# A feed-forward gate by ScalarE's x times sigmoid function, with one GpSimd product less for each half, and the second weight unit's remainders on VectorE

## The chip, the cores and the metric

One core of one Trainium2 chip runs the whole program. The metric is the device time of one execution in microseconds; a profiled execution gives the trace. In the profile PE is TensorE (matmul), PEld its weight load, DVE is VectorE, ACT is ScalarE, POOL is GpSimd, and SP (SyncE) issues the DMAs.

## The reference

A layer of a streaming encoder on x of 1024 frames by 1024 features: a mixing part (a recurrent mixer and band attention), a feed-forward part and a last gated embedding. The change lies in the feed-forward part:

```python
h2 = rmsnorm(x, norm_ffn_g[li])
x = x + (jax.nn.silu(h2 @ w_ffn_gate[li]) * (h2 @ w_ffn_up[li])) @ w_ffn_down[li]
h3 = rmsnorm(x, norm_ple_g[li])
x = x + jax.nn.sigmoid(h3 @ w_ple_gate[li]) * (p[li].astype(x.dtype) @ w_ple_proj[li])
```

Here silu(a) is a times sigmoid(a), and the hidden width D_FF is 2816. All inputs and outputs are float32.

## The kernel before

Activations lie with features on the 128 partitions and the 1024 frames along the free axis; most tiles are 128 x 1024 or a half of that, 128 x 512. Each float32 operand of a matmul is split into a high part (a cast to the matmul's own 32-bit type, `hi`) and a remainder (`lo`, the operand minus `hi`), and each product is made of three matmuls: hi by hi, hi by lo, lo by hi. In the trace the high parts of weights are `whi` or `wh`, the remainders `wlo` or `wl`. A remainder of weights is made by `wrest(engine, w, src)`, a subtraction of two SBUF tiles on the engine that it is given.

The feed-forward gate and up products are done by a Winograd form of Strassen's algorithm. The hidden features are cut into 22 units of 256, a unit of gate weights and one of up weights by turns. A unit takes seven products (`product(0)` to `product(6)`), each 12 matmuls of 128 x 128 by 128 x 512, that go into three PSUM banks b1, b2 and b3; b2 and b3 get a second product added, so DVE has to read what is there first (the sums u2 and u3). The seven weight blocks a11, s21 (two of them), a12, s3 and s4 are made from the unit's two raw tiles r1 and r2 by sums on DVE (tiles q), casts on ACT and remainders on DVE or POOL:

- `first_weights` makes those of the first unit. `strassen_weights(engine=None)` makes those of every later one, in steps that the caller advances with `next(more)`. Inside it G is the engine that was given, or POOL; a11, a12, s3 and s4 have their remainders made on G, s21 on V (DVE).
- `first_part` runs products 0 to 3 of the first gate unit, and `second_part` its products 4, 6 and 5, with the second unit's weights made between them: `more = self.strassen_weights()`.
- `ff_pairs` then runs the other 21 units by `strassen`; a unit's side stream (`side`) makes the next unit's weights, stores earlier results and issues the loads.

Order is fixed: V, A and G are wrappers (`Pinned`) that put each instruction behind the one recorded before it on the same engine, and PE and the loads on SP are chained in the same way. An engine that waits therefore holds up all that was recorded behind it. Where an instruction is issued through `nc.scalar` or `nc.vector` directly, a scheduler places it.

`unit_gate(c, half, ps)` takes a finished 128 x 512 result of a gate unit. `self.rb` holds each frame's factor of the norm, on all partitions. It makes g = ps times rb on DVE, sigmoid(g) on ACT into a temporary s (`t` in the trace), and then on POOL g times s and that times rb (the second rb is the up product's norm factor, applied ahead). `unit_up` multiplies the up product into it on DVE. There are 44 calls of `unit_gate`: four in `second_part` and 40 in the loop. Since these helpers record through `Pinned`, nearly all their instructions have line L54 in the trace, and matmuls L83; tiles tell them apart.

Rows that the text below uses: `q<-wr,wr`, `q<-q,wr`, `q<-wr` and `q<-wr,q` are a unit's weight sums on DVE; `s<-pm,rb` and `s<-t,rb` on DVE are the first line of `unit_gate`; `t<-pm,t` are the sums u2 and u3; `t<-s` on ACT is the gate function; `s<-s,t` and `s<-s,rb` on POOL are the two products.

After the loop come the product with the down weights (`ff_down`) and the last gated embedding (`ple`), which uses ACT's sigmoid.

Of the kernel before, what the change touches and what calls it, by code (L numbers as in the profile page):

```python
# [13 lines left out]
AF = mybir.ActivationFunctionType  # L14
ALU = mybir.AluOpType
# [41 lines left out]
class Trunk:  # L57
# [1244 lines left out]
    def second_part(self):  # L1302

        V, A = self.V, self.A
        b1, b2, b3 = self.banks
        self.strassen_load()
        next(self.embedded)
        self.norm_sums()
        for i in range(2):
            self.ffn_cast("T4", i)  # L1310
        u3 = self.stmp()
        V.tensor_tensor(u3, b2, self.p1, ALU.add)
        V.tensor_tensor(u3, b3, u3, ALU.add)
        next(self.embedded)
        drain(self.firsts)
        for i in range(2):
            self.ffn_rest("T4", i)
        self.gu = [self.slot() for _ in range(2)]
        drain(self.embedded)
        self.norm_rows()  # L1320
        self.unit_gate(1, 0, u3)
        more = self.strassen_weights()
        next(more)
        next(more)
        self.product(4, self.blocks("B21"), b1, False)
        next(more)
        self.unit_gate(0, 1, b1)
        next(more)
        self.product(6, self.blocks("B22"), b3, False)
        next(more)  # L1330
        V.tensor_tensor(self.u2, b3, self.u2, ALU.add)
        self.unit_gate(0, 0, self.u2)
        self.product(5, self.blocks("T4"), b2, False)
        next(more)
        u = self.stmp()
        V.tensor_tensor(u, b2, self.p1, ALU.add)
        self.unit_gate(1, 1, u)
        drain(more)
        self.sops = [self.blocks(kind) for kind in ("B11", "T2", "T1", "T3", "B21", "T4", "B22")]
# [31 lines left out]
    def unit_gate(self, c, half, ps):  # L1371
        V, A, G = self.V, self.A, self.G
        g = self.gu[c]
        hs = slice(half * HALF, half * HALF + HALF)
        s = self.stmp()
        V.tensor_tensor(g[:, hs], ps, self.rb[:, hs], ALU.mult)
        A.activation(s, g[:, hs], AF.Sigmoid)
        G.tensor_tensor(g[:, hs], g[:, hs], s, ALU.mult)
        G.tensor_tensor(g[:, hs], g[:, hs], self.rb[:, hs], ALU.mult)

    def unit_up(self, c, half, ps):
        hs = slice(half * HALF, half * HALF + HALF)
# [537 lines left out]
def drain(stream):  # L1920
    while True:
        try:
            next(stream)
        except StopIteration as e:
            return e.value
# [114 lines left out]
```

## Time and profile before

| | |
|---|---|
| median of 3 runs | 1595.65 us (1594.68 to 1601.39) |
| profiled execution, its own time | 1595.63 us |
| span of that execution in the trace | 1593.7 us |
| granted TensorE clock, mean | 0.998 |
| busy: PE, DVE, POOL, ACT | 1566.2, 1171.8, 783.6, 643.7 us |
| bytes moved by DMA | 230.52 MB, mean 145 GB/s |

The span is the time from the first to the last instruction in the trace; the time of an execution is 1.9 us longer. Busy times of different engines overlap, so their sum means nothing; what counts is which engine the end waits for at each stage. A row of a timeline gives start, length, engine, line, operation, output<-inputs, shape, count, and in brackets how long the engine was idle before it and who released it. The length of an operation includes the time in which it has begun and cannot go on.

### The profile page before, as it was taken

The numbers are of one execution on the slowest core, as the hardware profiler recorded it, in microseconds if no ns is written. First come the engines' busy times: TensorE is split into PE (matmuls) and PEld (weight loads), VectorE is DVE, ScalarE is ACT, GpSimd is POOL, SyncE is SP. The second block draws the span as 40 slices with busy tenths as digits, with TensorE's granted clock in tenths as the row PEclk, the third lists the DMA queues.
The fourth block names the chain that finished last, engine by engine and source line by source line (L and its number), as shares of the span: only waits on it lengthen the run. The fifth ranks groups of instructions, "written<-read, shape, count | busy, mean of one in ns | idle before, by whom it ended". The sixth has DMA issues, their size and how long they took to land.

```text
span 1593.7 us, 21834 instructions
## 1 busy us (share of the span) xinstructions
PE 1566.2 (98%) x8224; PEld 1309.3 (82%) x8224; DVE 1171.8 (74%) x1767; ACT 643.7 (40%) x1089; POOL 783.6 (49%) x445
## 2 busy tenths in 40 slices
PE   8999999999999999999999999999999999999997
PEld 6998989877888888888887788888888888888886
DVE  5656765489998777544898988888888866765658
ACT  5321221167677633421377322232222234445453
POOL 3422221257563064325230777777777764644554
PEclk9999999999999999999999999999999999999999
DMA  5101100245663465475244422233333268875334
GB/s 191 54 28 41 40 28 27 100 146 174 224 245 107 143 192 187 146 285 210 80 141 177 152 99 99 100 99 109 103 108 108 80 255 322 304 278 189 126 134 157
DMA packets 81897, 230.52 MB, mean 145 GB/s; under 512 B 9216, under 2 KB 9984, under 8 KB 81280
## 3 DMA queue, kind: packets, MB, share of 16 engines
q1 hardware_dynamic: 81648, 229.12, 40.6%
q8 instruction: 64, 1.05, 0.2%
q14 instruction: 41, 0.34, 0.1%
q10 hardware_dynamic: 144, 0.02, 0.0%
HBM read 163.82 MB, written 65.27 MB: 144 GB/s over the span
## 4 chain that ended last, share of the span: by engine, by line
PE 80%; DVE 9%; POOL 2%; ACT 2%; issue 2%; DMA 1%; SPq 0%; POOLq 0%; ACTq 0%; DVEq 0%
PE pm L83 77%; DVE s L54 5%; PE pm L86 2%; DVE m L54 2%; ACT s L54 1%; POOL wl L126 1%; POOL m L556 1%; DVE q L54 0%; DVE wl L126 0%; ACT wh L123 0%; DVE pm L54 0%; DMA d<-s 0%; DMA s<-in_oq 0%; POOL s L1075 0%; DMA wr<-d 0%
## 5 line engine op out<-in xcount | busy, mean ns | idle before, releaser
L83 PE MATMUL pm<-s,wh 128*128 128x512 f32 (+1 forms) x1712 | 532.1, 392 | 6.7 <-ACT wh L123 5.2
L83 PE MATMUL pm<-s,whi 128*128 128x512 f32 x1568 | 488.1, 392 | 1.2 <-DVE t L54 1.2
L126 POOL TENSOR_TENSOR wl<-wr,wh 128x1024 fp32r<-128x1024 f32 (+2 forms) x108 | 265.0, 2460 | 395.9 <-ACT wh L123 392.6
L83 PEld LDWEIGHTS pm<-s,wh 128*128 128x128 f32 x1712 | 320.1, 189 | 73.7 <-ACT wh L123 5.2
L83 PEld LDWEIGHTS pm<-s,whi 128*128 128x128 f32 x1568 | 294.7, 188 | 67.0 <-DVE t L54 1.7
L83 PE MATMUL pm<-s,wl 128*128 128x512 f32 (+1 forms) x856 | 334.1, 390 | 0.0
L54 DVE TENSOR_TENSOR s<-s,s 128x512 f32<-128x512 f32 (+4 forms) x213 | 257.3, 1236 | 90.5 <-ACT s L54 53.1
L83 PE MATMUL pm<-s,wlo 128*128 128x512 f32 x784 | 307.9, 393 | 0.9 <-DVE wlo L54 0.5
L83 PE MATMUL pm<-wh,s 128*128 128x256 f32 (+1 forms) x896 | 238.2, 340 | 0.0
L123 ACT CAST wh<-wr 128x1024 fp32r<-128x1024 f32 (+2 forms) x114 | 114.8, 1008 | 268.5 <-PE pm L83 143.9
L83 PEld LDWEIGHTS pm<-s,wl 128*128 128x128 f32 x856 | 161.5, 189 | 34.2 <-POOL wl L126 0.6
L83 PEld LDWEIGHTS pm<-s,wlo 128*128 128x128 f32 x784 | 147.4, 188 | 35.0 <-DVE wlo L54 1.1
L83 PEld LDWEIGHTS pm<-wh,s 128*128 128x128 f32 x896 | 154.6, 190 | 13.9 <-DVE s L341 0.2
L54 DVE TENSOR_TENSOR t<-pm,t 128x512 f32<-128x512 f32 x138 | 94.8, 687 | 88.3 <-PE pm L83 81.9
L54 DVE TENSOR_TENSOR s<-pm,s 128x512 f32<-128x512 f32 (+1 forms) x134 | 87.0, 680 | 86.4 <-PE pm L83 86.2
L83 PE MATMUL pm<-wl,s 128*128 128x256 f32 (+1 forms) x448 | 147.5, 329 | 0.4 <-POOL wl L126 0.4
L54 POOL TENSOR_TENSOR wlo<-wr,whi 128x512 fp32r<-128x512 f32 (+1 forms) x53 | 107.5, 2037 | 74.9 <-ACT whi L54 74.1
L54 ACT CAST whi<-q 128x512 fp32r<-128x512 f32 (+1 forms) x81 | 61.4, 757 | 153.4 <-DVE q L54 131.3
L54 POOL TENSOR_TENSOR s<-s,t 128x512 f32<-128x512 f32 x44 | 76.8, 1745 | 86.7 <-ACT t L54 86.7
L54 ACT CAST s<-s 128x1024 fp32r<-128x1024 f32 (+1 forms) x94 | 90.2, 980 | 61.8 <-DVE s L54 31.9
L54 POOL TENSOR_TENSOR wlo<-q,whi 128x512 fp32r<-128x512 f32 x52 | 87.9, 1691 | 45.7 <-ACT whi L54 31.9
L83 PEld LDWEIGHTS pm<-wl,s 128*128 128x128 f32 x448 | 85.3, 191 | 5.9 <-POOL wl L126 0.6
(147 smaller groups left out, 1949.2 us busy)
## 6 DMA issues: line engine op xcount, KB each, us to landing
d<-s SPq DMA_DIRECT2D x147, 256.0 KB, 3.4
s<-d SPq DMA_DIRECT2D x67, 512.0 KB, 5.9
wr<-d SPq DMA_DIRECT2D x36, 512.0 KB, 4.0
s<-in_wq SPq DMA_DIRECT2D x22, 512.0 KB, 5.4
wr<-in_sg SPq DMA_DIRECT2D x22, 512.0 KB, 3.9
wr<-in_su SPq DMA_DIRECT2D x22, 512.0 KB, 3.8
s<-in_x SPq DMA_DIRECT2D x21, 512.0 KB, 8.0
d<-s SPq DMA_DIRECT2D x18, 512.0 KB, 6.1
```

The source lines that it names most:

```text
L54: return lambda *a, **k: self.trunk.order(op(*a, **k), self.key)
L83: return self.order(self.nc.tensor.matmul(*a, **k))
L86: return self.order(self.nc.tensor.transpose(*a, **k))
L123: self.nc.scalar.copy(hi[:, c], raw[:, c])
L126: rest.tensor_tensor(lo[:, c], raw[:, c], f32(hi[:, c]), ALU.subtract)
L556: nc.gpsimd.tensor_tensor(ss, ss, self.mhalf[:, 0:8], ALU.pow)
```

## The change

ACT's function in `unit_gate` becomes Silu (x times sigmoid of x), so s already holds g times sigmoid(g), and POOL makes one product, s times rb, into g's place. In `second_part` the second unit's weights are made with `strassen_weights(V)`, so that the remainders of a11, a12, s3 and s4 of that one unit are recorded on DVE, in DVE's order; all later units are as before.

```diff
@@ second_part
         self.norm_rows()
         self.unit_gate(1, 0, u3)
-        more = self.strassen_weights()
+        more = self.strassen_weights(V)
         next(more)
         next(more)
         self.product(4, self.blocks("B21"), b1, False)
@@ unit_gate
         s = self.stmp()
         V.tensor_tensor(g[:, hs], ps, self.rb[:, hs], ALU.mult)
-        A.activation(s, g[:, hs], AF.Sigmoid)
-        G.tensor_tensor(g[:, hs], g[:, hs], s, ALU.mult)
-        G.tensor_tensor(g[:, hs], g[:, hs], self.rb[:, hs], ALU.mult)
+        A.activation(s, g[:, hs], AF.Silu)
+        G.tensor_tensor(g[:, hs], s, self.rb[:, hs], ALU.mult)
```

In the built program the orders of PE and, but for the four added remainders, of DVE are unchanged. ACT has two more table loads, one ahead of the first Silu and one ahead of the output stage's first sigmoid, where one cast has moved by a place; SP has two of the output stage's loads and stores exchanged.

## The prediction

> **What bounds the kernel now.** I read the page first (busy shares), then the stages, then the chain of waits, then the timelines of four engines around the one place where TensorE waits.
>
> ```profile
> PE 1566.2 (98%) x8224; PEld 1309.3 (82%) x8224; DVE 1171.8 (74%) x1767; ACT 643.7 (40%) x1089; POOL 783.6 (49%) x445
> ```
>
> The stages, as start:end, length, then busy time of PE, PEld, DVE, ACT, POOL:
>
> ```profile
> 843.00:896.00 53.00, 51.07 (x236) 41.30 (x235) 48.54 (x52) 35.77 (x56) 18.98 (x11) 1.00 0.49 179
> 896.00:1000.00 104.00, 104.00 (x454) 85.08 (x453) 89.89 (x85) 28.73 (x42) 74.55 (x43) 1.00 0.29 99
> 1200.00:1300.00 100.00, 100.00 (x436) 81.80 (x436) 78.95 (x73) 32.48 (x44) 76.50 (x43) 1.00 0.32 114
> ```
>
> and the chain that ended last (start, length, what):
>
> ```profile
> 882.67 2.23 DVE wlo L54
> ...
> 894.68 0.69 DVE t L54
> 895.41 613.76 PE pm L83 x2684
> ```
>
> The feed-forward loop (about 896 to 1300) is TensorE alone: busy for all of the 104.00 us and of the 100.00 us, and the chain is one piece of 613.76 us there. What POOL, ACT or DVE save inside the loop moves nothing. The change can only act ahead of 895.41, where the second unit's weights are made while the first is still multiplied. PE's own rows there:
>
> ```profile
> 885.04 0.63 PE L83 MATMUL pm<-s,whi 128*128 128x512 f32 x2
> 886.10 0.50 PE L83 MATMUL pm<-s,wlo 128*128 128x512 f32 x1 [0.43 <-POOL wlo L54]
> ...
> 893.78 0.39 PE L83 MATMUL pm<-s,wlo 128*128 128x512 f32 x1
> 895.41 0.73 PE L83 MATMUL pm<-s,whi 128*128 128x512 f32 x2 [1.24 <-DVE t L54]
> ```
>
> Two waits, 0.43 + 1.24 = 1.67 us, are all that the change can win. The first is for the remainder of the second unit's block a11, made by POOL; the second is for u2, the sum (t<-pm,t) that must read bank b2 before product 3 adds to it. DVE comes to u2 late because it has been busy without a gap. It is slow for one reason, seen by laying its rows beside POOL's:
>
> ```profile
> 872.76 1.22 DVE L54 TENSOR_TENSOR wlo<-wr,whi 128x1024 fp32r<-128x1024 f32 x1
> 879.56 0.68 DVE L54 TENSOR_TENSOR q<-wr,wr 128x512 f32<-128x512 f32 x1
> 880.27 0.69 DVE L54 TENSOR_TENSOR q<-q,wr 128x512 f32<-128x512 f32 x1
> 880.88 1.78 DVE L54 TENSOR_TENSOR q<-wr 128x512 f32<-128x512 f32 x1
> 882.59 2.31 DVE L54 TENSOR_TENSOR wlo<-q,whi 128x1024 fp32r<-128x1024 f32 x1
> 884.82 0.68 DVE L54 TENSOR_TENSOR s<-pm,rb 128x512 f32<-128x512 f32 x1
> 886.74 1.78 DVE L54 TENSOR_TENSOR q<-wr,q 128x512 f32<-128x512 f32 x1
> 888.45 0.68 DVE L54 TENSOR_TENSOR t<-pm,s 128x512 f32<-128x512 f32 x1
> 889.16 1.07 DVE L54 TENSOR_TENSOR s<-t,rb 128x512 f32<-128x512 f32 x1
> 890.16 2.90 DVE L54 TENSOR_TENSOR q<-wr,wr 128x512 f32<-128x512 f32 x1
> 893.09 1.67 DVE L54 TENSOR_TENSOR q<-q,wr 128x512 f32<-128x512 f32 x1
> 894.68 0.68 DVE L54 TENSOR_TENSOR t<-pm,t 128x512 f32<-128x512 f32 x1
> ```
> ```profile
> 875.55 1.27 POOL L54 TENSOR_TENSOR wlo<-wr,whi 128x512 fp32r<-128x512 f32 x1 [3.58 <-ACT whi L54]
> 880.38 1.74 POOL L54 TENSOR_TENSOR s<-s,t 128x512 f32<-128x512 f32 x1 [3.56 <-ACT t L54]
> ...
> 883.78 2.27 POOL L54 TENSOR_TENSOR wlo<-wr,whi 128x512 fp32r<-128x512 f32 x1
> 886.29 1.68 POOL L54 TENSOR_TENSOR s<-s,t 128x512 f32<-128x512 f32 x1 [0.25 <-ACT t L54]
> ...
> 889.65 2.86 POOL L54 TENSOR_TENSOR wlo<-wr,whi 128x1024 fp32r<-128x1024 f32 x1
> 892.46 1.75 POOL L54 TENSOR_TENSOR wlo<-q,whi 128x512 fp32r<-128x512 f32 x1
> ...
> 902.86 3.65 POOL L54 TENSOR_TENSOR wlo<-wr,whi 128x512 fp32r<-128x512 f32 x2
> ```
>
> A DVE operation with both inputs in SBUF takes 0.69 us (512 wide) or 1.22 us (1024) alone. Started under a POOL operation, it ends 0.55 us after that one: POOL 880.38 + 1.74 = 882.12, DVE 880.88 + 1.78 = 882.66; POOL 886.29 + 1.68 = 887.97, DVE 888.52; POOL 889.65 + 2.86 = 892.51, DVE 893.06; POOL 892.46 + 1.75 = 894.21, DVE 894.76. So one waits for the other to finish, whole, and POOL for DVE too (its product of 880.38 lasts from q's end, 880.96, to 882.12: 1.16). Operations that read PSUM (s<-pm,rb, t<-pm,s) stay at 0.68 under POOL. The excess of the six long rows from 880.88 to 893.09 is 1.09 + 1.09 + 1.09 + 0.38 + 2.21 + 0.98 = 6.84 us.
>
> **The change, part by part.** (1) One POOL product less for each half of a gate tile:
>
> ```profile
> L54 POOL TENSOR_TENSOR s<-s,t 128x512 f32<-128x512 f32 x44 | 76.8, 1745 | 86.7 <-ACT t L54 86.7
> ```
>
> 76.8 us leave POOL, 40 of these 44 in the loop, where PE covers them: worth 0 there. At the start of the loop POOL keeps four products with rb instead of eight products.
>
> (2) Four remainders (a11, a12, s3, s4; widths 512, 1024, 512, 512) go to DVE, in its order: a11 after the two q sums, a12 and s3 behind s<-pm,rb, s4 behind the last s<-t,rb. Alone: 3 x 0.69 + 1.22 = 3.29 us. The nearest rows bound them: alone 3.29, each under a POOL operation 3 x 1.78 + 2.31 = 7.65. They issue no DMA; they read the raw tiles sooner (a12 by 886.1, on POOL until 892.51), so that SP's next loads into these can only come earlier: 0.
>
> (3) A new wait. s4's remainder needs its high part, and ACT casts that only after the last gate function, which needs s<-t,rb:
>
> ```profile
> 876.32 1.20 ACT L227 COPY rb<-pm 128x512 f32<-128x512 f32 x2
> 879.67 0.63 ACT L54 ACTIVATE t<-s 128x512 f32<-128x512 f32 x1 [2.16 <-DVE s L54]
> 880.21 0.60 ACT L54 CAST whi<-wr 128x512 fp32r<-128x512 f32 x1
> ...
> 890.32 0.63 ACT L54 ACTIVATE t<-s 128x512 f32<-128x512 f32 x1 [2.77 <-DVE s L54]
> 890.86 0.60 ACT L54 CAST whi<-q 128x512 fp32r<-128x512 f32 x1
> ```
>
> s<-t,rb ended at 889.16 + 1.07 = 890.23, the cast at 891.46: DVE stands for 1.23 us, and queued behind it are the next unit's two q sums and then u2, for which PE waits.
>
> Now DVE's schedule with these, from 880.88 on, 0.6 us from one 512-wide start to the next, 0.7 if it needs the one before, 1.1 for 1024:
> - a11's remainder meets the first rb product (POOL 880.38, still released by 879.67 + 0.63) and ends at 882.66 as q did. PE wants it at 885.7: the 0.43 us wait goes.
> - q to 883.3, s21's remainder to 884.4, s<-pm,rb to 885.0, a12 to 886.1, with POOL idle until 885.8 (s<-pm,rb, then 0.63 of ACT).
> - s3: POOL's second product holds it up to 887.3, so 887.85. Then u2's sum and its product with rb to 889.1, q4 to 889.75, u to 890.35; before, u ended at 889.13, so DVE is 1.2 behind.
> - s<-t,rb meets the third rb product (from 890.0, 1.16 to 1.27 long) and ends at 891.7; ACT's 1.23 make 892.9; s4 meets the fourth, from 892.5 to 893.7, and ends at 894.2.
> - q and q then give u2's start at 895.4; but POOL, now without a queue, is free for the third unit's a11 at 894.0 (it took that up at 902.86 before), and one more meeting of 1.16 makes it 896.5.
>
> u2 ends at 896.2 to 897.2, PE's product 3 begins then and not at 895.41: +0.8 to +1.8 us. I take +1.5, since a11's cast (two short ACT operations behind s4's, so 894.0) comes ahead of q's start at 894.1. PE's own arrival 0.43 earlier is lost in that wait. After it DVE has slack: product 5 is the next to need a DVE read, two products (24 matmuls at 613.76/2684 = 0.229 us, 5.5 us) later.
>
> (4) Two table loads are added on ACT by the order of the built program: one right behind the rb copies, one ahead of the output stage's first sigmoids. Rows of a load here, and of the second place:
>
> ```profile
> 537.99 1.28 ACT L54 ACT_TABLE_LOAD   x1
> 539.28 2.01 ACT L54 ACTIVATE s<-s 128x1024 f32<-128x1024 f32 x2
> ...
> 1535.32 1.05 ACT L54 CAST s<-s 128x1024 fp32r<-128x1024 f32 x1
> 1539.84 2.38 ACT L54 ACTIVATE pm<-pm 128x512 f32<-128x512 f32 x4 [3.47 <-DVE pm L54]
> ```
>
> 1.28 us and the next operation 0.01 later. The first fits into the 2.16 us in which ACT waited ahead of 879.67 (copies end 877.52, load 878.80), the second into 3.47. Cost 0; without that cover 1.28 each. [...]
>
> (5) The new function itself: no row shows it. The nearest is the sigmoid, 0.63 us; the longest ACT form of this width lies under that of 1024 elements, 1.05. I take 0.63. Twice that would add 0.63 to DVE's wait in (3), less if faster: -0.2 to +0.6.
>
> Sum, on the profiled execution (span 1593.7, time 1595.63, 1.9 outside the span; the median of the runs is 1595.65, so the same): 1595.63 + 1.5 = 1597.1.
>
> **The rivals.**
> *The relief wins.* If POOL's four lost remainders and lost products take all 6.84 us of excess with them, against 3.29 + 1.23 added, u2 is 2.3 earlier; both PE waits go, 1.67: 1594.0. For it: POOL idles more. Against: each of the four rb products sits just where DVE reads SBUF.
> *DVE becomes the bound.* POOL, freed, pulls the third unit's remainders forward and each of the moved four is met: 7.65 + 1.23 added and no relief, +8.9: 1604.5. It decides over 0.5% only if POOL is as busy from 880 to 895 as now; against it, POOL must wait for ACT casts that stand behind the gate functions.
> *The table loads lie on the path.* If both hold up what follows in full, 2 x 1.28 on top of 1.5: 1599.7. [...] Against: the two idle times above.
> *The change does less than it says*: no sign; the built order has four DVE operations more and 48 on POOL fewer.
>
> **How the numbers follow.** About 0.5%, 8 us, is what can be told from no change. Forecast 0.62 (its own range 1596.4 to 1597.9), relief 0.22, DVE the bound 0.08, table loads 0.05, other 0.03. The range 1593.8 to 1600.0 holds the first, second and fourth; the three runs shown differ by more than these cases do (1594.68 to 1601.39), which takes off some of it. Slower by over 0.5%: half of the DVE case and a little for that spread, 0.07; faster needs 8 us where 1.67 are to be had: 0.02; the same 0.91.
>
> **What would show it.** The wait [0.43 <-POOL wlo] is gone; PE's wait for DVE t is 2.5 to 4 us and starts near 893.4; DVE has a gap of about 1.2 us ahead of the last of the four wlo; POOL in 896 to 1300 falls by about 70 us and PE stays fully busy there; two more table loads with no wait behind them. A PE wait at product 5 of the second unit, or any inside the loop, would make it wrong.

## The result, and the profile after

The changed kernel takes 1599.75 us (median of 15 runs, 1596.57 to 1606.78) against 1595.65 us before (15 runs beside it, 1593.27 to 1601.39). The ratio is 1.0028, with an interval of 1.002 to 1.0036: slower by 3.2 to 5.7 us. The profiled execution took 1599.67 us, with a span of 1597.9.

The page's first part, and the stages of the feed-forward loop (columns as before: start:end, length, busy time of PE, PEld, DVE, ACT and POOL, granted clock, DMA share, GB/s):

```profile
PE 1566.1 (98%) x8224; PEld 1309.0 (82%) x8224; DVE 1134.9 (71%) x1771; ACT 645.4 (40%) x1091; POOL 708.9 (44%) x397
```
```profile
843.00:896.00 53.00, 48.75 (x227) 39.66 (x226) 47.20 (x55) 36.57 (x56) 11.12 (x7) 1.00 0.49 179
896.00:1000.00 104.00, 104.00 (x446) 84.90 (x447) 75.59 (x84) 27.81 (x42) 51.27 (x28) 0.98 0.28 94
1200.00:1300.00 100.00, 100.00 (x436) 81.79 (x436) 74.98 (x78) 32.48 (x44) 60.05 (x32) 1.00 0.36 125
```

POOL is 74.7 us less busy and DVE 36.9 us, since its operations wait less for POOL's (`q<-wr,q` takes 2.33 us a row from 896 to 1300 before and 1.23 after, `q<-wr,wr` 1.78 and 1.20); both show in the loop, and PE is as full there as it was (436 matmuls in 100 us). Of these stages two differ for PE: the first, 2.3 us less busy, and the second, with the granted clock at 0.98 and 446 matmuls where there were 454. PE's timeline shows both within 10 us:

```profile
891.54 0.39 PE L83 MATMUL pm<-s,wlo 128*128 128x512 f32 x1
895.92 0.74 PE L83 MATMUL pm<-s,whi 128*128 128x512 f32 x2 [3.99 <-DVE t L54]
...
897.69 1.05 PE L83 MATMUL pm<-s,whi 128*128 128x512 f32 x2
898.54 0.63 PE L83 MATMUL pm<-s,wlo 128*128 128x512 f32 x1
898.97 1.05 PE L83 MATMUL pm<-s,whi 128*128 128x512 f32 x2
899.83 0.63 PE L83 MATMUL pm<-s,wlo 128*128 128x512 f32 x1
```

The wait for POOL's a11 (0.43 us) is gone. The wait ahead of product 3 has grown from 1.24 to 3.99 us. And behind it a group of three matmuls takes 1.28 us (897.69 to 898.97), not 0.7. Short stages of the changed kernel tell why:

```profile
895.90:897.00 1.10, 1.08 (x5) 0.90 (x6) 1.10 (x2) 1.10 (x2) 0.00 (x0) 1.00 0.00 0
897.00:900.50 3.50, 3.50 (x10) 2.72 (x9) 0.61 (x1) 0.69 (x2) 2.40 (x1) 0.51 0.46 150
900.50:905.00 4.50, 4.50 (x21) 3.71 (x21) 2.76 (x4) 0.23 (x1) 1.30 (x1) 1.00 0.01 2
```

The granted clock is 0.51 for 3.5 us (half clock, in what follows; the trace's clock records give 0.50 from 897.08 to 900.50), beginning a microsecond after PE resumed, and back at 1.00 after. Seven matmul starts lie 0.43 us apart where 0.23 is usual, so this costs 7 x 0.2 = 1.4 us.

DVE's rows, to lay beside the prediction's schedule (this execution runs 1.58 us earlier here: s<-t,rb at 877.38, not 878.96), ACT's first and last gate steps, and POOL's rows beside the end:

```profile
884.70 1.58 DVE L54 TENSOR_TENSOR wlo<-q,whi 128x512 fp32r<-128x512 f32 x1
...
888.13 0.68 DVE L54 TENSOR_TENSOR t<-pm,s 128x512 f32<-128x512 f32 x1
888.84 1.40 DVE L54 TENSOR_TENSOR s<-t,rb 128x512 f32<-128x512 f32 x1
891.50 1.37 DVE L54 TENSOR_TENSOR wlo<-q,whi 128x512 fp32r<-128x512 f32 x1 [1.26 <-ACT whi L54]
892.79 1.75 DVE L54 TENSOR_TENSOR q<-wr,wr 128x512 f32<-128x512 f32 x1
894.58 0.69 DVE L54 TENSOR_TENSOR q<-q,wr 128x512 f32<-128x512 f32 x1
895.18 0.68 DVE L54 TENSOR_TENSOR t<-pm,t 128x512 f32<-128x512 f32 x1
```
```profile
875.99 1.28 ACT L54 ACT_TABLE_LOAD   x1
878.10 0.63 ACT L54 ACTIVATE t<-s 128x512 f32<-128x512 f32 x1 [0.82 <-DVE s L54]
...
890.33 0.63 ACT L54 ACTIVATE t<-s 128x512 f32<-128x512 f32 x1 [2.00 <-DVE s L54]
890.86 0.60 ACT L54 CAST whi<-q 128x512 fp32r<-128x512 f32 x1
```
```profile
891.03 1.29 POOL L54 TENSOR_TENSOR s<-t,rb 128x512 f32<-128x512 f32 x1 [1.34 <-ACT t L54]
892.54 1.45 POOL L54 TENSOR_TENSOR wlo<-wr,whi 128x512 fp32r<-128x512 f32 x1 [0.22 <-ACT whi L54]
```

The gap of 1.26 us ahead of s4's remainder is the wait that the change adds. That remainder and the next unit's first q sum then take 1.37 and 1.75 us under POOL's fourth product and POOL's remainder of the third unit's a11, and u2 ends at 895.86; PE starts 0.06 later.

From a matmul ahead of the second unit (884.58 before, 883.04 after) to one of the same place in the order just behind that unit (the 92nd, counting both), PE needed 23.12 us before and 26.74 after: +3.62 us, which accounts for most of the difference, and lies in its interval. Two other differences between the two traces are not of the same standing: the start and middle of the program went 1.5 us faster in the second, and a wait near 1510 (for the norm's sums of the last stage) grew from 0.53 to 2.00 us.

### The profile page after: what moved, and what is told of

Same layout as the page of the kernel before. It is cut to its first block, busy times and chain, and to the rows that moved or that the text cites. A ratio compares the mean times of both kernels' runs of the same rounds, so it can differ in the third digit from the quotient of the medians.

```text
span 1597.9 us, 21791 instructions
## 1 busy us (share of the span) xinstructions
PE 1566.1 (98%) x8224; PEld 1309.0 (82%) x8224; DVE 1134.9 (71%) x1771; ACT 645.4 (40%) x1091; POOL 708.9 (44%) x397
## 5 line engine op out<-in xcount | busy, mean ns | idle before, releaser
L54 POOL TENSOR_TENSOR wlo<-wr,whi 128x512 fp32r<-128x512 f32 (+1 forms) x51 | 117.6, 2314 | 99.6 <-ACT whi L54 96.1
L54 POOL TENSOR_TENSOR wlo<-q,whi 128x512 fp32r<-128x512 f32 x50 | 79.5, 1589 | 89.2 <-ACT whi L54 76.7
L54 POOL TENSOR_TENSOR s<-t,rb 128x512 f32<-128x512 f32 x44 | 70.3, 1607 | 97.9 <-ACT t L54 97.9
```

The costliest lines, as they stand in the source:

```text
L54: return lambda *a, **k: self.trunk.order(op(*a, **k), self.key)
```

## The experiments

Theory A: the second unit's remainders on DVE make u2 late, PE waits for it, and half clock follows. Rivals: the late wait near 1510 and the output stage (B), and the Silu function with its table loads (C). The expectations count PE's wait from where its next matmul would have started, 0.23 us after the last; what is 1.24 and 3.99 us in the brackets of a row is 1.4 and 4.1 us there.

**The changed kernel again.** 

> The changed kernel as it is, a second trace of it. Theory A (the second unit's remainders on DVE make u2 late, PE waits about 4.1 us ahead of product 3 and then runs some 3 us at half clock): +3.5 to +4.5 us against before, the same wait of 3.8 to 4.4 us, matmul starts 0.43 us apart behind it. Theory B (the extra time is the wait for the norm's sums near 1510, which grew from 0.53 us to 2.01 us, and the output stage): the wait ahead of product 3 may vary, but the one near 1510 is about 2 us again.

Measured: 1600.42 us against 1596.77, ratio 1.0018 (1.0007 to 1.0029). The stage rows, 870 to 890 and behind the wait:

```profile
870.00:873.50 3.50, 3.24 (x23) 2.95 (x22) 2.56 (x4) 3.50 (x5) 0.47 (x1) 1.00 0.17 67
873.50:877.00 3.50, 3.50 (x11) 2.70 (x10) 3.46 (x4) 2.45 (x5) 2.11 (x1) 0.53 0.22 83
877.00:890.00 13.00, 13.00 (x66) 10.97 (x65) 12.27 (x14) 9.65 (x15) 2.82 (x3) 1.00 0.93 314
901.50:905.00 3.50, 3.50 (x9) 2.80 (x10) 1.66 (x2) 1.34 (x2) 2.02 (x1) 0.58 0.44 147
```

PE's wait was 2.75 us here, not 3.8 to 4.4, but there were two spells of half clock. The earlier one follows no long wait, but the norm's sums, 16 matmuls one column wide. It held PE back about 1.4 us (an estimate: seven starts, as above) while DVE went on, so that u2 was less late; and it held up the copies of rb, behind which the first table load then lay on the path for 0.6 us (DVE waited that long for a11's cast). The wait near 1510 was 0.53 us again, and this execution took 1602.95 us, no less than the 1599.67 of the first: theory B is not needed for the loss. That wait grew in the first trace and in three of the kernels below (the remainders alone on DVE, two and four sums more). In the first trace a load of raw weights, issued at the same place, took 5.0 us to land and not 3.3, so that POOL's remainders of them came later and met four operations of DVE ahead of the norm's sums (`s<-s,q`, 6.54 us together and not 5.06). Why the load took longer is not settled, nor whether the slower kernels have a part in it: four of their six traces have the longer wait, and none of the eight others.

**The new gate alone.** The diff's part in `unit_gate` only. 

> The new gate alone: Silu and one POOL product, the second unit's remainders on POOL as before. Theory A: DVE has before's operations and meets fewer POOL ones, PE's wait ahead of product 3 is below 1.2 us, the wait for a11's remainder goes, no half clock; -0.5 to -1.7 us against before. Theory C (the Silu function or its two table loads cost the time): +3 to +4.5 us.

Measured: 1596.95 us against 1596.77, ratio 0.9994 (0.998 to 1.0007). Theory C is out. A's time is neither shown nor excluded (-3.2 to +1.1 us), but what it said of the trace missed: PE still waited for u2, 1.93 us, and half clock followed (granted 0.65 over the 4.86 us behind it). Four POOL products fewer did not relieve DVE; the first two rows below met the remainders of a12 and s3, which POOL now reached sooner, and the third a product:

```profile
888.92 2.18 DVE L54 TENSOR_TENSOR s<-t,rb 128x512 f32<-128x512 f32 x1
891.02 1.78 DVE L54 TENSOR_TENSOR q<-wr,wr 128x512 f32<-128x512 f32 x1
892.83 1.65 DVE L54 TENSOR_TENSOR q<-q,wr 128x512 f32<-128x512 f32 x1
```

**The remainders on DVE alone.** Only `strassen_weights(V)`. 

> The other part alone: the sigmoid and two POOL products as before, the second unit's remainders on DVE. Theory A: DVE has the four added operations, the wait for ACT's cast of s4, and all eight POOL products to meet: PE waits 4 to 6 us ahead of product 3, half clock behind it, +4 to +6 us against before. Theory C: no change against before, within 1 us.

Measured: 1603.44 us against 1596.77, ratio 1.0038 (1.0024 to 1.0052). PE waits 5.18 us and half clock follows:

```profile
900.26 1.22 PE L83 MATMUL pm<-s,whi 128*128 128x512 f32 x2 [5.18 <-DVE t L54]
```

The whole loss is in this part (3.8 to 8.3 us, from six runs). That the new gate takes a little of it back is what the waits say (5.18 us here, 3.99 and 2.75 with it); the intervals of the times overlap.

**s4's remainder back on POOL.**

```diff
-        rest(G, s4, q4)
+        rest(self.G, s4, q4)
```


> The changed kernel with s4's remainder alone given back to POOL (a11, a12 and s3 stay on DVE). Theory A: DVE's gap of 1.26 us for ACT's cast and the operation of 1.37 us behind it go, so that PE's wait falls from 4.1 to 1.5 to 2.5 us, and no half clock follows; 0 to +1.5 us against before. If the number of operations on DVE and not the wait for the cast makes the delay: PE's wait 3.4 to 3.6 us, +3 us.

Measured: 1596.39 us, ratio 0.9996 (0.9987 to 1.0006). With three of the four remainders still on DVE the loss is gone. No wait is left ahead of product 3 in its trace, for two reasons: q and q meet no POOL operation when they come 1.3 us earlier (0.68 and 0.69 us), and an early spell of half clock (from 872.12; the mean granted clock of this execution is 0.995, against 0.998 in the trace before) held PE back. In the trace of this kernel with two products exchanged, below, which has no such spell, u2 ends 0.9 us after PE could have begun product 3, so that without the spell about this much of wait is to be expected.

**s4's remainder alone on DVE.** The kernel before, with `rest(V, s4, q4)` for the second unit. 

> The kernel before with s4's remainder alone on DVE for the second unit (a11, a12 and s3 on POOL, the sigmoid and two POOL products as before). If DVE's wait for the cast of s4 is what makes u2 late: a gap of about 1.2 us on DVE ahead of that remainder, PE's wait ahead of product 3 grows from 1.4 to 2.7 to 3.5 us, half clock behind it, +2 to +4 us against before, most of what all four cost. If the number of operations counts: a quarter of it, about +1 us.

Measured: 1600.76 us against 1597.48, ratio 1.0024 (1.0012 to 1.0036): within the noise, one operation of the four costs as much as all. DVE's rows:

```profile
891.38 1.07 DVE L54 TENSOR_TENSOR s<-t,rb 128x512 f32<-128x512 f32 x1
893.71 1.56 DVE L54 TENSOR_TENSOR wlo<-q,whi 128x512 fp32r<-128x512 f32 x1 [1.26 <-ACT whi L54]
895.20 1.78 DVE L54 TENSOR_TENSOR q<-wr,wr 128x512 f32<-128x512 f32 x1
```

The gap is again 1.26 us. In this trace half clock came ahead of the second unit (granted 0.54 from 871.90 to 875.50), which hid part of DVE's delay, so that PE's wait was 2.05 us only, and no half clock followed that.

**All four on DVE, s4's cast earlier.** The same operations as the changed kernel; one step is recorded ahead of the last gate step in place of behind it.

```diff
         V.tensor_tensor(u, b2, self.p1, ALU.add)
+        drain(more)
         self.unit_gate(1, 1, u)
-        drain(more)
```


> The changed kernel with s4's cast and remainder recorded ahead of the last gate step in place of behind it; all four remainders stay on DVE. If the wait for the cast is the cause: no gap on DVE ahead of s4's remainder, PE's wait falls from 4.1 to 0.8 to 1.8 us, no half clock or seldom, -1 to +0.5 us against before. If four more operations on DVE are: PE's wait about 2.9 us and half clock, +2.5 to +3 us.

Measured: 1596.05 us, ratio 0.9998 (0.9985 to 1.0011), the loss is gone. DVE and PE:

```profile
889.18 0.68 DVE L54 TENSOR_TENSOR t<-pm,s 128x512 f32<-128x512 f32 x1
890.03 1.27 DVE L54 TENSOR_TENSOR wlo<-q,whi 128x512 fp32r<-128x512 f32 x1 [0.17 <-ACT whi L54]
891.22 0.68 DVE L54 TENSOR_TENSOR s<-t,rb 128x512 f32<-128x512 f32 x1
891.82 0.68 DVE L54 TENSOR_TENSOR q<-wr,wr 128x512 f32<-128x512 f32 x1
```
```profile
893.88 0.73 PE L83 MATMUL pm<-s,whi 128*128 128x512 f32 x2 [0.92 <-DVE t L54]
```

The gap is 0.17 us, the q sum takes 0.68 and not 1.75, PE waits 0.92 us, and the clock stays at 1.00. So neither the number of operations on DVE nor their kind makes the delay, but the place of one of them behind a cast that itself stands behind the gate function.

**The wait alone, by doses.** The kernel before with the second unit's sum u2 made again, two or four times, by operations that read PSUM (`t<-pm,t`), which POOL does not hold up: 0.69 us a row from 896 to 1300 in the trace before, with POOL busy for 300 of the 404 us; here the three take 2.13 us together.

```diff
         u2 = add(tmp(), p1, b2)
+        for _ in range(dose):
+            add(u2, p1, b2)
```


> The kernel before with the sum u2 of the second unit made three times in place of once (two more DVE operations of 0.6 to 0.7 us that read PSUM, nothing else), which lengthens PE's wait ahead of product 3 from 1.4 to 2.7 us. If a microsecond of wait costs a microsecond and no more: +1.3 us. If half clock follows waits of over 2 us, as after the waits of 2.1 to 5.3 us in four traces: +2.7 us, matmul starts 0.43 us apart for some 3 us.

> As with two more sums, but four: PE's wait 4.0 us, as long as in the changed kernel, with nothing else of the change in it. If the wait with the half clock behind it makes the changed kernel slower: +3.5 to +4.5 us against before, as the changed kernel. If only the wait counts: +2.6 us. If the cause lies elsewhere (POOL, ACT, the output stage): under +2.6 us.

Measured: with two, 1600.30 us against 1595.04, ratio 1.0032 (1.002 to 1.0045), above both numbers expected; with four, 1601.56 us, ratio 1.0035 (1.0022 to 1.0048). Each trace is of the slowest run of its kernel (1604.28 and 1603.30 us). PE in the kernel with two, and its stages:

```profile
899.54 1.19 PE L83 MATMUL pm<-s,whi 128*128 128x512 f32 x2 [2.77 <-DVE t L54]
900.53 0.63 PE L83 MATMUL pm<-s,wlo 128*128 128x512 f32 x1
```
```profile
899.50:905.50 6.00, 5.96 (x14) 4.73 (x15) 3.56 (x3) 0.62 (x1) 5.92 (x5) 0.50 0.00 0
905.50:910.00 4.50, 4.50 (x20) 3.65 (x20) 4.09 (x4) 0.00 (x0) 4.50 (x3) 0.98 0.38 118
```

1.5 us more of wait cost about 5 us. Half clock held for 6 us behind it (14 matmuls, where 4.50 us hold 20 or 21), which is worth 14 x 0.2 = 2.8 us. A longer wait, with nothing else of the change, gives a loss of the changed kernel's size or more (3.5 to 7.7 us with four sums, against 3.2 to 5.7). With four sums PE waited only 3.34 us, since an early spell had held it back too (the mean granted clock of this execution is 0.994, the lowest of the profiled ones); the two more cost about 1 us more, which is not clear of the noise. Both traces also have the longer wait near 1510, and that with four a third spell of half clock behind it, so that the figures hold more than the one wait.

**Filling the wait.** Product 4 of the second unit ahead of its product 3 (`swap` is set for that unit alone), in three kernels: the changed one, that with s4's remainder on POOL, and the new gate alone.

```diff
+        if swap:
+            product(4, b1, False)
         product(3, b2, False)
...
-            product(4, b1, False)
+            if not swap:
+                product(4, b1, False)
```


> The changed kernel with the second unit's product 4 moved ahead of its product 3 (order 0, 1, 2, 4, 3, 5, 6), so that PE has 2.7 us of work where it waited for u2. Theory A (the wait, and the half clock behind it): PE waits 0.5 to 1.6 us ahead of product 3 and a new 0.8 us ahead of product 5, whose sum u3 now has no product to hide behind; no half clock there; 0 to +1.5 us against before, so 2.5 to 4 us under the changed kernel. If the time lies anywhere else: as the changed kernel, +3 to +4.5 us.

> s4's remainder given back to POOL, and product 4 ahead of product 3. Theory A: no wait ahead of product 3 even in executions in which DVE is late, but 0.8 us ahead of product 5; -1 to +0.5 us against before, so no gain over the kernel with s4's remainder on POOL alone.

> The new gate with all remainders on POOL, and the second unit's product 4 ahead of its product 3. The wait of 2.1 us seen with the new gate alone is filled with 2.7 us of work and no half clock follows; 0.8 us of wait ahead of product 5: -0.9 us against before, and 0 to 1.5 us under the new gate alone.

Measured: 1596.75 us, ratio 1.0007 (0.9997 to 1.0018); 1594.94 us, ratio 0.9997 (0.9989 to 1.0006); 1597.68 us, ratio 0.9996 (0.9985 to 1.0007). The waits are as expected, 0.94 us ahead of product 3 in the first and none in the others; each has a new one of 0.85 or 0.86 us ahead of product 5, and no half clock behind either:

```profile
896.45 0.73 PE L83 MATMUL pm<-s,whi 128*128 128x512 f32 x2 [0.94 <-DVE t L54]
...
900.36 0.73 PE L83 MATMUL pm<-s,whi 128*128 128x512 f32 x2 [0.86 <-DVE t L54]
```

With the changed kernel's DVE and POOL as they were, work for PE in the wait takes away most of the loss (-0.5 to +2.9 us are left). The other two are no faster than the same kernels without the exchange, as far as the runs can tell.

The mean granted clock of all runs, not only of the traced ones, bears out the part of half clock; a spell of 3.41 us takes 0.0011 off it. It is 0.9957 with the changed kernel, 0.9947 with the remainders alone on DVE and 0.9963 with s4's back on POOL, against 0.9964 before; 0.9951 and 0.9952 with two and four sums more, against 0.9971; and 0.9958 with s4's remainder alone on DVE, 0.9968 with its cast earlier, against 0.9964. The changed kernel with product 4 ahead is the exception: 0.9960 against 0.9971, though its trace has no spell. What its other runs met is not known.

**a11 and a12 alone on DVE.** s3 and s4 on POOL, the rest as changed. 

> The changed kernel with a11 and a12 alone on DVE, s3 and s4 on POOL. DVE has two operations fewer than the changed kernel and no wait for the cast; PE waits neither for a11's remainder nor, or under 0.5 us, for u2: -0.8 to -1.7 us against before. If POOL is then late with s3's remainder, which product 3 needs: a wait for POOL wlo of about 1 us there, 0 against before.

Measured: 1595.53 us against 1597.48, ratio 0.9995 (0.9983 to 1.0007). PE waits neither for a remainder nor for u2 around the second unit. But its trace has a spell of half clock ahead of that unit (seven starts 0.43 us apart from 870.45), which holds PE back, as half of the fourteen traces have, with and without the change. Neither this kernel nor another is shown to beat the kernel before: the 1.67 us in question are a tenth of a per cent.

## Why the prediction was right or wrong

- **Where the change acts: right.** The loop is PE's alone (100.00 us busy of 100.00), and POOL's 69.8 us less in 896 to 1300 (300.4 to 230.6 in the stages) moved nothing. The first unit's end is where it was decided.
- **DVE's schedule: right to its last step.** With the 1.58 us added, s3's remainder ended at 887.86 (887.85 predicted), u at 890.39 (890.35), s<-t,rb at 891.82 (891.7), s4's remainder at 894.45 (894.2). That one operation waits for the other's end, and that the freed POOL comes early to a11 (892.54 + 1.58 = 894.12, predicted 894.0), held.
- **u2's end: just past the edge.** 897.44 in the same frame, predicted 896.2 to 897.2, and taken short of the upper end though a11's early start was seen; PE's product 3 came 2.1 us later than before, not 1.5.
- **The step that failed is from "PE's product 3 begins then" to "+0.8 to +1.8 us".** The sum priced the wait by its length, and put what comes behind it at nothing without a reason. A wait of 4 us, which "what would show it" itself foresaw as 2.5 to 4, was followed by half clock, worth 1.4 us in the first trace and 2.8 (14 starts) with two sums more. The term of +1.5 measures 3.62 in the trace, of which 2.1 are the later start and 1.4 half clock, and 3.2 to 5.7 in the runs. The granted clock of 1.00 in the stages shown of the trace before gave no price for it.
- **That 1599.75 us still lies in the range of 1593.8 to 1600.0 is luck.** The upper end was there for the table loads (1599.7) and for the spread of the runs; neither made the time.
- **The new wait (3): right in mechanism and size,** 1.23 predicted, 1.26 measured in each of the traces with s4's remainder last on DVE; and the two kernels around s4 show that it makes the loss.
- **The table loads: nothing in the changed kernel's first trace** (the first takes 1.28 us, then ACT is 0.82 idle until DVE releases the gate function; the second 1.28, then 2.18 idle), as forecast. The first load came onto the path for 0.6 us where half clock had made the rb copies late (0.62 in the changed kernel's second trace, in which the gate function started 0.01 us behind the load).
- **The Silu function: right,** 0.63 us.
- **"The relief wins": not here.** With the gate alone the relief did not come, since POOL's remainders moved up into the freed time. With all four remainders on DVE and s4's cast earlier, PE's wait did fall from 1.24 to 0.92 us and that for a11 went, but no gain is shown in the times.

## What to carry to other kernels

Before an operation moves to an engine with a full queue, look at what its inputs wait for: a short operation behind a cast on another engine, which stands behind this engine's own last result, costs the round trip for all that is queued behind it (1.26 us here). Where the wait cannot be avoided, record the cast earlier (the gap fell to 0.17 us), or give TensorE a product to do in the meantime (its wait was 0.94 us then, not 3.99 or 2.75). Of this case's seven waits of TensorE of 1.93 to 5.18 us ahead of product 3, six had half clock behind them: price such a wait with that (here an estimated 1.4 us for a spell of seven slow starts), not by its length alone.

## What the runs showed of the hardware

In the fourteen traces half clock followed each wait ahead of product 3 of 2.75 us or more (2.75, 2.77, 3.34, 3.99, 5.18), one of two near 2 us (1.93 yes, 2.05 no), and none of 1.24 us or less. In seven of the fourteen it came behind the norm's sums (granted 0.53 from 873.50 to 877.00 in the changed kernel's second trace, 0.54 from 871.90 to 875.50 with s4's remainder alone on DVE), where PE waits 0.3 us at most (0.26 in the trace before) but computes 16 matmuls one column wide in 1.84 us.

The clock's records suggest what decided it. Apart from the start and the end of the program, a spell lasts 3.41 us (897.08 to 900.50 in the first trace), or twice that (granted 0.50 for all of the 6.00 us from 899.50 with two sums more). The changes lie whole multiples of 3.413 us apart: in the first trace the records begin at 9.62 and half clock begins at 897.08 and, at the program's end, at 1589.99, which is 260 and 203 times that; in the trace before they begin at 14.26 and half clock at 1587.80, 461 times; in the changed kernel's second trace its two spells begin near 873.7 and 901.0, 8 times. So in these traces the clock changes at fixed steps. The wait of 1.93 us lay within one step, and half clock began with the next; that of 2.05 us was cut by the end of a step (stage rows, the new gate alone first, s4's remainder alone on DVE behind it):

```profile
892.66:896.07 3.41, 1.48 (x7) 0.92 (x6) 3.38 (x4) 2.22 (x4) 3.41 (x3) 1.00 0.19 72
896.07:899.48 3.41, 3.41 (x10) 2.66 (x9) 2.32 (x2) 0.44 (x1) 3.41 (x2) 0.50 0.00 0
```
```profile
895.72:899.13 3.41, 1.53 (x7) 0.94 (x5) 3.38 (x3) 0.45 (x1) 3.33 (x3) 1.00 0.47 154
899.13:902.55 3.42, 3.25 (x14) 2.67 (x15) 3.42 (x4) 1.88 (x3) 3.34 (x3) 1.00 0.00 0
```

Laid out like this, a spell followed each wait ahead of product 3 of which 1.93 us or more fell into one step (2.25 us in the first trace, in the step from 893.67 to 897.08), and none of which 1.88 us or less did. From the first of the norm's 16 narrow matmuls to the next wide one PE takes 2.10 us (867.27 to 869.37 in the trace before): the spell came in the seven traces in which all of it fell into one step, and in none of the seven in which at most 1.85 us did (1.78 before, 1.43 in the changed kernel's first trace). So what seems to count is the time without wide matmuls within one step, with the border between 1.88 and 1.93 us here; this is read from the fourteen traces, and no run was made to test it. The changed kernel shows the early spell in its second trace and not in its first. A spell of seven slow starts (0.43 us apart, not 0.23) is worth about 1.4 us, an estimate.
